# PSUM banks dealt out anew in a hybrid attention and matrix-memory block

## The chip, the cores and the metric

The kernel runs on one core of a Trainium2 chip. Its time is the device time of one execution in microseconds (us); lower is better. In tables and rows, PE is TensorE's matmuls, PEld its weight loads, DVE is VectorE, ACT is ScalarE, POOL is GpSimd, and SP is the engine that issues most of the DMA transfers; a name such as SPq or PEq is that engine's instruction queue. L12 is line 12 of the kernel before the change. In the changed kernel the same statement stands one line higher from line 316 on, since one line is gone; the text keeps the numbers of before, except where rows of the new order are shown.

## The reference

The input x is 1024 tokens by 1024 channels. It is normalised and multiplied by one wide matrix, whose columns feed two branches and their gates:

```
xn = rmsnorm(x);  da_q, da_k, da_v, da_z, ml_q, ml_k, ml_v, ml_o, ml_z, ml_i, ml_f, gate_a, gate_m = split(xn @ w_in)

# differential attention, 8 heads, two score maps p of 64 columns each
probs[p] = softmax(mask(q[p] @ k[p].T / 8 + bias))        # block-causal mask, 64-token chunks
y_a = rmsnorm((probs[0] - lam * probs[1]) @ v) * silu(da_z)

# mLSTM, 8 heads, chunkwise: decayed state C = C * decay + (w * k).T @ v
h = (scores @ v + w_inter * (q @ C)) / max(|den|, exp(-m))
y_m = sigmoid(ml_o) * layernorm(h) * silu(ml_z)

merged = sigmoid(gate_a) * (y_a @ w_pa) + sigmoid(gate_m) * (y_m @ w_pm)
out = rmsnorm(x + merged @ w_out)
```

All in float32. The kernel keeps that precision on TensorE by splitting each operand of the large products into two 16-bit parts, a high and a low half, and running three matmuls for each product (high by high, high by low, low by high).

## The kernel before

**Units.** The wide product is done in units of 256 columns. A unit's weights are loaded (`load`, L226, on SP's queue) into two tiles `wt`, of which three exist, and prepared (`prep`): ScalarE squares them (L245), VectorE adds the sums (L159), a matmul with a matrix of ones (L165) adds over the partitions, VectorE derives a power-of-two scale `sb` from it (`pow2`, L135 to L139), and four times ScalarE writes a high half (L257) and VectorE a low half (L259). Then TensorE multiplies: `plain_unit` (L329 to L331, 96 matmuls of 512 columns, called projection matmuls below) or `rows_unit` (L358 to L360, 192 matmuls of 256 columns). Each unit has 32 steps (`yield`). In each step one step of the next unit's preparation is written, too.

**Sides.** Beside the units of a phase runs a side: attention of the head before, or `mlstm` of the head before. A side is cut into named pieces, and a table (`PLAN_A` for the first seven attention heads, `PLAN_C` for the eighth, others for mlstm) gives each piece the slot of its writing. In `attention`, `q` and `r` are the scores (L812) and softmax (L822, L826) of a row block of 128 tokens for the two maps. `r` also combines them (L832 to L837), splits the result into halves (L844 on ScalarE, L845 on VectorE) and transposes it by a DMA (L847, tile z). `v` is the product of the transposed block with v (L855 to L857, then a square on ScalarE, L858); `f` makes the norm factors of four row blocks on GpSimd (L862 to L864); `o` scales their products (L870, reads PSUM); `t` turns the rows for the later projection (L547 to L549).

**PSUM.** Eight banks in four pools: `pp` three for the units, `psb` one tile of two banks for scores, `pmi` two for everything small, `pvp` one for the products with v. Four row blocks share one bank of `pvp`: it is taken by row blocks 0 and 4.

```
        def pv(i):
            if i % 4 == 0:
                ops[i // 4] = v_ps()
```

**What sets the order.** The code's order gives priorities. A scheduler of the programming layer then places the instructions of each engine in a fixed order by its own model, and lets a tile wait until a buffer of its pool is free. Each engine and each DMA queue executes its own list in order.

**The start.** `startup` transposes x block by block into PSUM (L396) and splits it (L398 on ScalarE, L399 on VectorE), woven with the first unit's preparation. `tables` writes the bias table to DRAM (L430, L432); its reader is `strip` (L584). The first unit is q and k of head 0, whose halves are copied to Q and K by DMA (L608, L610), the second v and z of head 0. `if_proj` writes the matrix-memory gates (L468, L471 on ScalarE, L472 on SP).

Of the kernel before, what the change touches and what calls it, by code (L numbers as in the profile page):

```python
# [17 lines left out]
P = 128  # L18
# [14 lines left out]
OFF_GATE = (9232, 10256)  # L33
BIG = 3.0e38
RING = 15
PLAN_A = [(0, 'q0'), (0, 'r0'), (0, 'q1'), (3, 'r1'), (4, 'q2'), (5, 'r2'), (9, 'q3'), (9, 'r3'), (9, 'q4'), (10, 'v0'), (14, 'v1'), (16, 'r4'), (17, 'q5'), (18, 'v2'), (19, 'r5'), (21, 'q6'), (24, 'r6'), (25, 'q7'), (27, 'r7'), (28, 'v3'), (29, 'v4'), (29, 'v5'), (30, 'f0'), (30, 'o0'), (31, 'v6'), (31, 'v7'), (42, 't0'), (55, 'f1'), (55, 'o1'), (55, 't1')]
PLAN_C = [(0, 'q0'), (0, 'r0'), (6, 'q1'), (7, 'r1'), (7, 'q2'), (9, 'r2'), (16, 'q3'), (19, 'r3'), (19, 'q4'), (19, 'r4'), (19, 'v0'), (22, 'v1'), (22, 'v2'), (25, 'q5'), (28, 'r5'), (29, 'q6'), (31, 'v3'), (32, 'v4'), (33, 'r6'), (37, 'q7'), (38, 'f0'), (38, 'r7'), (46, 'o0'), (52, 'v5'), (52, 'v6'), (63, 'v7'), (64, 'f1'), (67, 'o1'), (82, 't1'), (83, 't0')]
PLAN_M = [(0, '00gate'), (0, '01k0'), (2, '02k1'), (4, '03s0'), (5, '04s1'), (8, '05e0'), (9, '06p0'), (11, '07e1'), (13, '08p1'), (14, '09c0'), (19, '10g00'), (19, '11g01'), (20, '12g02'), (21, '13cp0'), (22, '14bs0'), (22, '15g10'), (25, '16g11'), (25, '17g12'), (26, '18cp1'), (30, '19bs1'), (30, '20g20'), (30, '21g21'), (31, '22cp2'), (32, '23bs2'), (33, '24ch'), (37, '25n0'), (47, '26t0'), (50, '27n1'), (55, '28t1')]
PLAN_N = [(0, '00gate'), (1, '01k0'), (1, '02k1'), (8, '03s0'), (10, '04s1'), (13, '05e0'), (13, '06p0'), (15, '07e1'), (16, '08p1'), (22, '09c0'), (25, '10g00'), (26, '11g01'), (26, '12g02'), (26, '13cp0'), (30, '14bs0'), (31, '15g10'), (36, '16g11'), (37, '17g12'), (40, '18cp1'), (42, '19bs1'), (43, '20g20'), (44, '21g21'), (53, '22cp2'), (54, '23bs2'), (59, '24ch'), (61, '25n0'), (67, '26t0'), (70, '27n1'), (71, '28t1')]
# [9 lines left out]
def block_kernel(ctx, tc, x, norm_w, w_in, lam, subln_w, rel_bias, conv_w, conv_b, b_if,  # L49
# [3 lines left out]
    PSUM = bass.MemoryType.PSUM  # L53
# [6 lines left out]
    dram = ctx.enter_context(tc.tile_pool(name="dram", bufs=1, space=bass.MemoryType.DRAM))  # L60
    pp = ctx.enter_context(tc.tile_pool(name="pp", bufs=3, space=PSUM))
    psb = ctx.enter_context(tc.tile_pool(name="psb", bufs=1, space=PSUM))
    pmi = ctx.enter_context(tc.tile_pool(name="pmi", bufs=2, space=PSUM))
    pvp = ctx.enter_context(tc.tile_pool(name="pvp", bufs=1, space=PSUM))

    uid = [0]

# [166 lines left out]
    def prep(w, rowscale=None, keep=False):  # L234
        wd = w.width
        if rowscale is not None:
            g.tensor_tensor(w.wt[0], w.wt[0], rowscale[:, 0:4].unsqueeze(2).to_broadcast([P, 4, wd]), op=ALU.mult)
            yield
            for k in range(4, 8):
                s.activation(w.wt[k // 4][:, k % 4, :], w.wt[k // 4][:, k % 4, :], AF.Copy, scale=rowscale[:, k:k + 1])  # L240
            yield
        ss = sm(cols=2, p="wss")
        for k in range(2):
            j = junk(4 * wd).rearrange("p (a b) -> p a b", a=4)
            s.activation(j, w.wt[k], AF.Square, accum_out=ss[:, k:k + 1])  # L245
            yield
        yield
        yield
        w.sb = sm(p="sb")
        w.isb = sm(p="isb", bufs=8)  # L250
        fnorm_finish(ss, w.sb, w.isb)
        yield
        w.parts = {}

        def split(name, src, dst):
            w.parts[name] = dst
            s.activation(dst[0], src, AF.Copy, scale=w.sb)  # L257
            yield
            v.scalar_tensor_tensor(dst[1], src, w.sb, dst[0], op0=ALU.mult, op1=ALU.subtract)  # L259
            yield  # L260

        if keep:
            t = [R(F16, [P, KC, 256], p="wo") for _ in range(2)]
        for k in range(0, KC, 2):
            src = w.wt[k // 4][:, k % 4:k % 4 + 2, :]
            if keep:
                dst = (t[0][:, k:k + 2, :], t[1][:, k:k + 2, :])
            else:
                u = wparts([2, 256])
                dst = (u[:, 0, :, :wd], u[:, 1, :, :wd])  # L270
            yield from split(k // 2, src, dst)
# [25 lines left out]
    class Unit:  # L297
# [13 lines left out]
        def start_prep(self):  # L311
            if self.prepping is None:
                self.finish_load()
                self.prepping = prep(self.w, self.rowscale and self.rowscale(), self.keep)
                self.left = 16

        def prep_step(self):
            return spent(self.prepping)
# [71 lines left out]
    def startup(th):  # L390
        for kc in range(KC):
            if kc % 2 == 0:
                X[th, kc // 2] = xtile("X")
            tp = m_ps()
            for tt in range(4):
                te.transpose(tp[:, tt * P:(tt + 1) * P], xts[th * 4 + tt][:, kc * P:(kc + 1) * P], ident)  # L396
            hi, lo = x_src(kc, th)
            s.activation(hi, tp, AF.Copy, scale=nws[:, kc:kc + 1])  # L398
            v.scalar_tensor_tensor(lo, tp, nws[:, kc:kc + 1], hi, op0=ALU.mult, op1=ALU.subtract)  # L399
            yield  # L400
# [49 lines left out]
    def if_proj():  # L450
# [11 lines left out]
            yield  # L462
        t = R(shape=[32, S], p="gif")
        for th in range(2):
            gps = m_ps()
            for i in range(KC):
                for k in range(2):
                    te.matmul(gps[:32, :], parts[:, i, :], x_src(i, th)[k], start=(i + k == 0),  # L468
                              stop=(i + k == KC))
                yield  # L470
            s.activation(t[:, HS[th]], gps[:32, :], AF.Copy, scale=sig[:32, :])  # L471
# [3 lines left out]
    def if_gates():  # L475
# [51 lines left out]
        s.dma_start(dec_d[0:1, :].rearrange("o (h c) -> (o h) c", c=NT), dec)  # L527
        s.dma_start(decb, dec_d[0:1, :].to_broadcast([P, H * NT]))
        yield
        cps = m_ps()  # L530
        for k, t in enumerate((a, ws, en)):
            for c in range(NT):
                o = (k * NT + c) * H
# [354 lines left out]
    def mlstm(h):  # L888
# [6 lines left out]
        kw = R(shape=[P, NT, P], p="kw")  # L895
        for th in range(2):
            n = 4 - th
            tp = m_ps()
            for j in range(n):
                c = th * 4 + j  # L900
                te.transpose(tp[:, j * P:(j + 1) * P], k[:, c * P:(c + 1) * P], ident)
# [320 lines left out]
```

## Time and profile before

| | us |
|---|---|
| median of 3 runs (lowest to highest) | 1435.84 (1435.15 to 1436.73) |
| the profiled execution, its own time | 1435.78 |
| its span, from first to last instruction | 1433.9 |
| mean granted TensorE clock | 0.995 |
| TensorE busy, DVE busy, ACT busy, POOL busy | 1380.6, 848.0, 735.0, 157.5 |
| share of the chain that ended last: PE, DVE, ACT, DMA, POOL | 77%, 9%, 4%, 4%, 3% |

Matmuls overlap, so TensorE's busy time is the union of theirs. A row of the timeline gives start, duration, engine, line, operation, output and inputs, shape, count, and in brackets how long the engine stood before it and what ended that. A row of the waits gives who waited on whom, total us, times and the longest. A row of busy times by stretch gives the stretch, its length, the busy time of PE, PEld, DVE, ACT and POOL with counts, the granted clock (1.00 is full), the DMA share and GB/s.

### The profile page before, as it was taken

How to read it: one execution, taken by the hardware profiler on the slowest of the kernel's cores; microseconds unless marked ns; L12 is line 12 of the kernel's file. 1: busy time of each engine (PE TensorE's matmuls, PEld its weight loads, DVE VectorE, ACT ScalarE, POOL GpSimd, SP SyncE). 2: the span in 40 equal slices, each digit the busy share in tenths (PEclk: the TensorE clock that was granted, in tenths of full speed). 3: DMA queues.
4: the chain of work that ended last, by engine and by line, in shares of the span. 5: the costliest groups of instructions: out<-in, count | busy, mean ns of one | idle time of the engine just before them, and what ended most of it. 6: DMA issues, size and time to landing. Idle time of an engine off the chain costs nothing.

```text
span 1433.9 us, 25050 instructions
## 1 busy us (share of the span) xinstructions
PE 1380.6 (96%) x9650; PEld 913.3 (64%) x9650; DVE 848.0 (59%) x2310; ACT 735.0 (51%) x1533; POOL 157.5 (11%) x215
## 2 busy tenths in 40 slices
PE   6989999999999999999999999999999999999997
PEld 3656575665756655444486787778769675444786
DVE  6276868677686756533445674775866564233633
ACT  7276556565566667832353444443435344644542
POOL 2001010010100100100102020220211200122004
PEclk9999999999999999999999999999999999999999
DMA  6456355463554645543321313231232135534303
GB/s 200 68 142 140 83 107 124 104 141 82 114 121 91 136 95 130 163 149 125 96 74 60 104 31 101 47 87 47 66 97 75 60 86 158 168 103 162 118 16 118
DMA packets 232585, 150.14 MB, mean 105 GB/s; under 512 B 117297, under 2 KB 209730, under 8 KB 232466
## 3 DMA queue, kind: packets, MB, share of 16 engines
q1 hardware_dynamic: 218450, 123.28, 35.0%
q10 hardware_dynamic: 14016, 25.27, 5.3%
q8 instruction: 75, 1.23, 0.3%
q14 instruction: 44, 0.36, 0.1%
HBM read 90.12 MB, written 18.55 MB: 76 GB/s over the span
## 4 chain that ended last, share of the span: by engine, by line
PE 77%; DVE 9%; ACT 4%; DMA 4%; POOL 3%; issue 3%; SPq 0%; POOLq 0%; DVEq 0%; ACTq 0%
PE pp L329 14%; PE pp L331 14%; PE pp L330 14%; PE pp L360 8%; PE pp L358 8%; PE pp L359 8%; PE psb L812 3%; DVE z L822 3%; DMA z<-z 2%; ACT z L826 1%; DMA qw<-rows_d 1%; DVE wp L259 1%; PE psb L908 1%; PE pvp L855 1%; DVE hl L600 1%
## 5 line engine op out<-in xcount | busy, mean ns | idle before, releaser
L358 PE MATMUL pp<-wp,X 128*128 128x256 f16 x1280 | 349.7, 273 | 0.0
L359 PE MATMUL pp<-wp,X 128*128 128x256 f16 x1280 | 349.7, 273 | 0.0
L360 PE MATMUL pp<-wp,X 128*128 128x256 f16 x1280 | 349.7, 273 | 0.0
L329 PE MATMUL pp<-X,wp 128*128 128x512 f16 x768 | 291.7, 380 | 0.3 <-ACT wp L257 0.3
L331 PE MATMUL pp<-X,wp 128*128 128x512 f16 x768 | 291.3, 379 | 0.6 <-DVE wp L259 0.6
L330 PE MATMUL pp<-X,wp 128*128 128x512 f16 x768 | 291.8, 380 | 0.0
L257 ACT ACTIVATE wp<-wt,sb 128x512 f16<-128x512 f32 x208 | 136.9, 711 | 105.4 <-DVE sb L138 70.6
L331 PEld LDWEIGHTS <-wp 128*128 128x128 f16 x1024 | 100.0, 98 | 119.7 <-DVE wp L259 1.2
L245 ACT ACTIVATE junk<-wt 128x1024 bf16<-128x1024 f32 x112 | 118.1, 1055 | 100.0 <-DMA wt<-in_w_in_dram 89.7
L329 PEld LDWEIGHTS <-wp 128*128 128x128 f16 x1024 | 100.2, 98 | 103.0 <-issue 1.7
L330 PEld LDWEIGHTS <-wp 128*128 128x128 f16 x1024 | 100.1, 98 | 97.1
L259 DVE SCALAR_TENSOR_TENSOR wp<-wt,sb,wp 128x512 f16<-128x512 f32 x208 | 150.5, 760 | 14.4 <-ACT wp L257 12.8
L359 PEld LDWEIGHTS <-X 128*128 128x128 f16 x1280 | 125.3, 98 | 18.4 <-issue 2.4
L358 PEld LDWEIGHTS <-X 128*128 128x128 f16 x1280 | 125.4, 98 | 16.8 <-issue 0.8
L360 PEld LDWEIGHTS <-X 128*128 128x128 f16 x1280 | 125.3, 98 | 14.6
L826 ACT ACTIVATE z<-z,mx 128x256 f32<-128x256 f32 (+7 forms) x128 | 99.0, 773 | 61.7 <-DVE mx L825 46.1
L822 DVE CUSTOM_DVE_ANT_0 z<-psb,BB,negc 128x256 f32<-128x256 f32 (+7 forms) x128 | 104.1, 813 | 19.7 <-PE psb L812 19.4
L331 PE MATMUL pp<-Y,wp 128*128 128x512 f16 x256 | 97.1, 379 | 0.0
L330 PE MATMUL pp<-Y,wp 128*128 128x512 f16 x256 | 97.1, 379 | 0.0
L329 PE MATMUL pp<-Y,wp 128*128 128x512 f16 x256 | 97.1, 379 | 0.0
L649 DVE SCALAR_TENSOR_TENSOR acc<-up,wcol,acc 128x512 f32<-128x512 f32 x96 | 78.0, 827 | 27.4 <-POOL acc L650 24.5
L812 PE MATMUL psb<-K,Q 128*128 128x512 f16 (+3 forms) x384 | 83.5, 326 | 7.8 <-DMA K<-hl 4.6
(245 smaller groups left out, 2012.1 us busy)
## 6 DMA issues: line engine op xcount, KB each, us to landing
wt<-in_w_in_dram SPq DMA_DIRECT2D x128, 256.0 KB, 3.4
wt<-in_w_in_dram SPq DMA_DIRECT2D x24, 512.0 KB, 3.9
K<-hl SPq DMA_DIRECT2D x32, 256.0 KB, 3.7
gate_d<-tg ACTq DMA_DIRECT2D x32, 256.0 KB, 2.2
xt<-in_x_dram SPq DMA_DIRECT2D x8, 512.0 KB, 5.2
Q<-hl SPq DMA_DIRECT2D x32, 128.0 KB, 2.4
wt<-in_w_pa_dram SPq DMA_DIRECT2D x8, 512.0 KB, 5.4
ft<-gate_d ACTq DMA_DIRECT2D x16, 256.0 KB, 2.8
```

The source lines that it names most:

```text
L245: s.activation(j, w.wt[k], AF.Square, accum_out=ss[:, k:k + 1])
L257: s.activation(dst[0], src, AF.Copy, scale=w.sb)
L259: v.scalar_tensor_tensor(dst[1], src, w.sb, dst[0], op0=ALU.mult, op1=ALU.subtract)
L329: te.matmul(ps, wh, xh, start=(start and i == 0), stop=False, **kw)
L330: te.matmul(ps, wh, xl, start=False, stop=False, **kw)
L331: te.matmul(ps, wl, xh, start=False, stop=(stop and i == n - 1), **kw)
L358: te.matmul(ps[:, o], xh[:, t], wh, start=i == 0, stop=False)
L359: te.matmul(ps[:, o], xh[:, t], wl, start=False, stop=False)
L360: te.matmul(ps[:, o], xl[:, t], wh, start=False, stop=i == KC - 1)
L812: te.matmul(sp[:, c:e], Q[:, p, i * P:(i + 1) * P], K[p][:, j, c:e], start=(j == 0), stop=(j == 1))
L822: v.tensor_tensor_reduce(z[:, :n], sp[:, :n], bb[:, S - n:], negc, BIG, op0=ALU.add, op1=ALU.min, accum_out=mx)
L826: s.activation(z[:, :n], z[:, :n], AF.Exp, bias=mx, scale=-1.0, accum_out=rr[:, 2 * i + p:2 * i + p + 1])
```

## The change

Of the eight banks, `pvp` gets two instead of one and `pmi` one instead of two. The transposes at the start, the gate products, and mlstm's transposes and state products move from `pmi` to `pvp`; `pmi` keeps the norm sums and three small uses at the start. The norm sum of a preparation stands three steps later. In `PLAN_A` the products with v of row blocks 6 and 7 stand two and four slots later. An unused line (`self.left`) is gone.

```
-PLAN_A = [... (30, 'f0'), (30, 'o0'), (31, 'v6'), (31, 'v7'), (42, 't0') ...]
+PLAN_A = [... (30, 'f0'), (30, 'o0'), (33, 'v6'), (35, 'v7'), (42, 't0') ...]
...
-    pmi = ctx.enter_context(tc.tile_pool(name="pmi", bufs=2, space=PSUM))
-    pvp = ctx.enter_context(tc.tile_pool(name="pvp", bufs=1, space=PSUM))
+    pmi = ctx.enter_context(tc.tile_pool(name="pmi", bufs=1, space=PSUM))
+    pvp = ctx.enter_context(tc.tile_pool(name="pvp", bufs=2, space=PSUM))
...
             s.activation(j, w.wt[k], AF.Square, accum_out=ss[:, k:k + 1])
             yield
-        yield
-        yield
+        for _ in range(5):
+            yield
         w.sb = sm(p="sb")
...
-            tp = m_ps()          # startup, transposes of x
+            tp = v_ps()
...
-            gps = m_ps()         # if_proj
+            gps = v_ps()
...
-        cps = m_ps()             # if_gates
+        cps = v_ps()
...
-            tp = m_ps()          # mlstm, transposes of k
+            tp = v_ps()
...
-            cp = m_ps()[:, :P + 1]   # mlstm, state
+            cp = v_ps()[:, :P + 1]
```

The scheduler's order changes with it at many places. Three are shown: the start, the start of attention (two engines), and one attention head.

*The start, VectorE.* X halves are L399 (now L398), x scaled is L387 (L386), low halves of the first weights L259. Before:

```order
L399 SCALAR_TENSOR_TENSOR X_214<-pmi_240,nws_134,X_214 128x512
L381 ISA junk_250,xss_249<-xt_104 128x1024
L399 SCALAR_TENSOR_TENSOR X_256<-pmi_257,nws_134,X_256 128x512
L387 TENSOR_SCALAR xt_104<-xt_104,xrs_252 128x1024
L259 SCALAR_TENSOR_TENSOR wp_247<-wt_156,sb_222,wp_247 128x512
L387 TENSOR_SCALAR xt_105<-xt_105,xrs_268 128x1024
L399 SCALAR_TENSOR_TENSOR X_256<-pmi_272,nws_134,X_256 128x512
L387 TENSOR_SCALAR xt_106<-xt_106,xrs_284 128x1024
L399 SCALAR_TENSOR_TENSOR X_288<-pmi_289,nws_134,X_288 128x512
L259 SCALAR_TENSOR_TENSOR wp_279<-wt_156,sb_222,wp_279 128x512
```

After:

```order
L398 SCALAR_TENSOR_TENSOR X_214<-pvp_229,nws_134,X_214 128x512
L380 ISA junk_237,xss_236<-xt_104 128x1024
L398 SCALAR_TENSOR_TENSOR X_243<-pvp_244,nws_134,X_243 128x512
L386 TENSOR_SCALAR xt_104<-xt_104,xrs_239 128x1024
L386 TENSOR_SCALAR xt_105<-xt_105,xrs_254 128x1024
L398 SCALAR_TENSOR_TENSOR X_243<-pvp_258,nws_134,X_243 128x512
L386 TENSOR_SCALAR xt_106<-xt_106,xrs_279 128x1024
L398 SCALAR_TENSOR_TENSOR X_283<-pvp_284,nws_134,X_283 128x512
L259 SCALAR_TENSOR_TENSOR wp_291<-wt_156,sb_265,wp_291 128x512
L398 SCALAR_TENSOR_TENSOR X_283<-pvp_293,nws_134,X_283 128x512
L259 SCALAR_TENSOR_TENSOR wp_309<-wt_156,sb_265,wp_309 128x512
```

The first low half of weights stood before the scaling of x block 105; now it stands four operations further on, behind the low half of pvp_284.

*The start of attention, TensorE.* L165 is the norm sum of the third unit, L812 (now L811) the score products of head 0: psb_923 and psb_931 are row block 0 in the two maps, psb_944 is row block 1; pp_843 is the last quarter of the second unit, 48 matmuls. Before:

```order
L360 MATMUL pp_790<-wp_523,X_394 128x256
L165 MATMUL pmi_705<-s_703,ones_91 128x1
L812 MATMUL psb_923<-K_426,Q_425 128x128
...
L812 MATMUL psb_931<-K_427,Q_425 128x128
...
L358 MATMUL pp_843<-wp_492,X_325 128x256
...
L812 MATMUL psb_944<-K_426,Q_425 128x256
```

After:

```order
L359 MATMUL pp_784<-wp_536,X_394 128x256
L165 MATMUL pmi_728<-s_726,ones_91 128x1
L811 MATMUL psb_923<-K_426,Q_425 128x128
...
L357 MATMUL pp_843<-wp_505,X_325 128x256
...
L811 MATMUL psb_931<-K_427,Q_425 128x128
...
L811 MATMUL psb_944<-K_426,Q_425 128x256
```

The second score product stood right behind the first; now the 48 matmuls of pp_843 stand between, and row block 1 follows with 7 projection matmuls of the third unit done instead of 3.

*The same place, ScalarE.* gif is the gates' product (L471, now L470), wp the high halves of the third unit, wt_669 and the tile after it the fourth unit's weights, mx_927 and mx_934 the softmax of row block 0 in the two maps. Before:

```order
L245 ACTIVATE junk_681,wss_672<-wt_532 128x1024
L471 ACTIVATE gif_600<-pmi_601,sig_443 32x512
L471 ACTIVATE gif_600<-pmi_619,sig_443 32x512
L567 ACTIVATE vr_644<-pp_650 128x256
L257 ACTIVATE wp_718<-wt_458,sb_701 128x512
L257 ACTIVATE wp_738<-wt_458,sb_701 128x512
...
L257 ACTIVATE wp_753<-wt_532,sb_701 128x512
L257 ACTIVATE wp_768<-wt_532,sb_701 128x512
...
L826 ACTIVATE z_926,rr_920<-z_926,mx_927 128x128
...
L826 ACTIVATE z_926,rr_920<-z_926,mx_934 128x128
L245 ACTIVATE junk_962,wss_961<-wt_669 128x1024
```

After:

```order
L245 ACTIVATE junk_681,wss_672<-wt_545 128x1024
L257 ACTIVATE wp_741<-wt_458,sb_724 128x512
...
L257 ACTIVATE wp_791<-wt_545,sb_724 128x512
L470 ACTIVATE gif_600<-pvp_601,sig_443 32x512
L470 ACTIVATE gif_600<-pvp_619,sig_443 32x512
...
L562 ACTIVATE tz_643<-pp_711,hs_640 128x256
L825 ACTIVATE z_926,rr_920<-z_926,mx_927 128x128
L245 ACTIVATE junk_962,wss_961<-wt_669 128x1024
L245 ACTIVATE junk_967,wss_961<-wt_806 128x1024
L562 ACTIVATE tz_643<-pp_843,hs_640 128x256
```

The four high halves moved ahead of the gates, and both squares (L245) of the fourth unit moved ahead of the second softmax of row block 0. On VectorE the small sum over these squares stands ahead of the scan of psb_931.

*An attention head (the second), VectorE.* z_1984 and z_2003 belong to row block 6, z_2022 and z_2038 to row block 7, on_2151 is the scaling of row blocks 0 to 3 (L870, now L869), hl halves of the next head's k. Before:

```order
L600 SCALAR_TENSOR_TENSOR hl_1880<-pp_1975,hl_1880 128x512
L834 SCALAR_TENSOR_TENSOR nbeta_2008<-rr_1694,nlam_141,rc_1695 128x1
L837 SCALAR_TENSOR_TENSOR z_1984<-z_2003,nbeta_2008,z_1984 128x896
L822 ISA z_2038,mx_2039<-psb_2033,BB_95,negc_899 128x1024
L845 TENSOR_TENSOR z_2003<-z_1984,z_2003 128x896
L870 SCALAR_TENSOR_TENSOR on_2151<-pvp_1855,fac_2147,tz_1289 128x128 x2
L832 RECIPROCAL rc_1695<-rr_1694 128x2
L870 SCALAR_TENSOR_TENSOR on_2151<-pvp_1855,fac_2147,tz_1289 128x128
L834 SCALAR_TENSOR_TENSOR nbeta_2043<-rr_1694,nlam_141,rc_1695 128x1
L870 SCALAR_TENSOR_TENSOR on_2151<-pvp_1855,fac_2147,tz_1289 128x128
L837 SCALAR_TENSOR_TENSOR z_2022<-z_2038,nbeta_2043,z_2022 128x1024
```

After:

```order
L836 SCALAR_TENSOR_TENSOR z_1984<-z_2003,nbeta_2008,z_1984 128x896
L821 ISA z_2038,mx_2039<-psb_2033,BB_95,negc_899 128x1024
L844 TENSOR_TENSOR z_2003<-z_1984,z_2003 128x896
L599 SCALAR_TENSOR_TENSOR hl_1874<-pp_1975,hl_1874 128x512
L831 RECIPROCAL rc_1695<-rr_1694 128x2
L869 SCALAR_TENSOR_TENSOR on_2151<-pvp_1850,fac_2147,tz_1289 128x128
L833 SCALAR_TENSOR_TENSOR nbeta_2043<-rr_1694,nlam_141,rc_1695 128x1
L869 SCALAR_TENSOR_TENSOR on_2151<-pvp_1850,fac_2147,tz_1289 128x128
L836 SCALAR_TENSOR_TENSOR z_2022<-z_2038,nbeta_2043,z_2022 128x1024
L869 SCALAR_TENSOR_TENSOR on_2151<-pvp_1850,fac_2147,tz_1289 128x128 x2
```

The hl half moved from ahead of row block 6's combination to behind its low half, and the small factor nbeta_2043 of row block 7 from behind the third scaling to behind the first. On TensorE, 6 instead of 37 projection matmuls (L358 to L360) stand between the products of row blocks 3 and 4 of this head, and 66 instead of 71 between those of row blocks 3 and 7. On ScalarE the squares L858 of row blocks 4 and 5 stand ahead of row block 7's high half as one of them did before, with one L245 more.

More of the change, by code (lines that the diff above doesn't have):

```diff
@@ L35 @@
 RING = 15
-PLAN_A = [(0, 'q0'), (0, 'r0'), (0, 'q1'), (3, 'r1'), (4, 'q2'), (5, 'r2'), (9, 'q3'), (9, 'r3'), (9, 'q4'), (10, 'v0'), (14, 'v1'), (16, 'r4'), (17, 'q5'), (18, 'v2'), (19, 'r5'), (21, 'q6'), (24, 'r6'), (25, 'q7'), (27, 'r7'), (28, 'v3'), (29, 'v4'), (29, 'v5'), (30, 'f0'), (30, 'o0'), (31, 'v6'), (31, 'v7'), (42, 't0'), (55, 'f1'), (55, 'o1'), (55, 't1')]
+PLAN_A = [(0, 'q0'), (0, 'r0'), (0, 'q1'), (3, 'r1'), (4, 'q2'), (5, 'r2'), (9, 'q3'), (9, 'r3'), (9, 'q4'), (10, 'v0'), (14, 'v1'), (16, 'r4'), (17, 'q5'), (18, 'v2'), (19, 'r5'), (21, 'q6'), (24, 'r6'), (25, 'q7'), (27, 'r7'), (28, 'v3'), (29, 'v4'), (29, 'v5'), (30, 'f0'), (30, 'o0'), (33, 'v6'), (35, 'v7'), (42, 't0'), (55, 'f1'), (55, 'o1'), (55, 't1')]
 PLAN_C = [(0, 'q0'), (0, 'r0'), (6, 'q1'), (7, 'r1'), (7, 'q2'), (9, 'r2'), (16, 'q3'), (19, 'r3'), (19, 'q4'), (19, 'r4'), (19, 'v0'), (22, 'v1'), (22, 'v2'), (25, 'q5'), (28, 'r5'), (29, 'q6'), (31, 'v3'), (32, 'v4'), (33, 'r6'), (37, 'q7'), (38, 'f0'), (38, 'r7'), (46, 'o0'), (52, 'v5'), (52, 'v6'), (63, 'v7'), (64, 'f1'), (67, 'o1'), (82, 't1'), (83, 't0')]
@@ L314, in start_prep @@
                 self.prepping = prep(self.w, self.rowscale and self.rowscale(), self.keep)
-                self.left = 16
         def prep_step(self):
```

## The prediction

> **What bounds the kernel now.** I read the page's first table, then TensorE's part of the table of waits, then the busy times by stretch, and last the timeline of the stretches where TensorE stands. Busy shares first:
>
> ```profile
> span 1433.9 us, 25050 instructions
> PE 1380.6 (96%) x9650; PEld 913.3 (64%) x9650; DVE 848.0 (59%) x2310; ACT 735.0 (51%) x1533; POOL 157.5 (11%) x215
> 760.00:880.00 120.00, 120.00 (x911) 91.61 (x910) 78.13 (x223) 52.12 (x106) 16.21 (x20) 1.00 0.26 71
> 160.00:220.00 60.00, 56.73 (x444) 38.07 (x442) 43.94 (x126) 37.44 (x86) 4.61 (x8) 1.00 0.54 110
> ```
>
> In the last two rows the first number after the stretch is its length, the second TensorE's busy time. In 760 to 880 us (the matrix-memory heads) TensorE never stands, so nothing is to be won there. In one attention head (160 to 220) it stands 3.3 us of 60. What it stands for:
>
> ```profile
> PE pvp L855 <- DVE on L870: 12.0, 8, 1.6
> PE psb L812 <- DMA K<-hl: 4.6, 2, 2.5
> PE pvp L855 <- DMA z<-z: 4.2, 5, 1.1
> PE pmi L165 <- DVE s L159: 1.6, 7, 0.2
> ```
>
> Columns: total us, times, longest. The first row is the single bank of pvp: the fifth product with v (row block 4, L855) waits until the scaling L870 has read the first four out of it, once per head. The third is the last product with v, which waits for its transposed probabilities. The fourth is the norm sum, a matmul placed before its input is there. The second is one place, the start of attention. Together 22.4 us; the kernel is TensorE's work plus these, so a gain is read in TensorE's waits alone.
>
> **The change part by part.** One head in detail (the second; the others look alike):
>
> ```profile
> 176.73 1.28 DVE L822 CUSTOM_DVE_ANT_0 z<-psb,BB,negc 128x1024 f32<-128x1024 f32 x1 [1.11 <-PE psb L812]
> 180.96 0.35 ACT L858 ACTIVATE junk<-pvp,rc 128x128 bf16<-128x128 f32 x1
> 181.30 1.14 ACT L826 ACTIVATE z<-z,mx 128x1024 f32<-128x1024 f32 x1
> 183.51 0.20 POOL L864 TENSOR_TENSOR fac<-fac,rc 128x4 f32<-128x4 f32 x1
> 183.75 0.61 DVE L870 SCALAR_TENSOR_TENSOR on<-pvp,fac,tz 128x128 f32<-128x128 f32 x2 [1.53 <-POOL fac L864]
> 184.98 1.28 DVE L837 SCALAR_TENSOR_TENSOR z<-z,nbeta,z 128x1024 f32<-128x1024 f32 x1
> 185.12 0.22 PE L855 MATMUL pvp<-vr,z 128*128 128x128 f16 x1 [1.59 <-DVE on L870]
> 186.57 1.04 ACT L844 ACTIVATE z<-z 128x1024 f16<-128x1024 f32 x1
> 187.65 1.23 DVE L845 TENSOR_TENSOR z<-z,z 128x1024 f16<-128x1024 f32 x1 [0.58 <-ACT z L844]
> 187.72 0.27 PE L358 MATMUL pp<-wp,X 128*128 128x256 f16 x1
> 187.83 0.27 PE L359 MATMUL pp<-wp,X 128*128 128x256 f16 x1
> 188.90 4.91 DMA z<-z
> 193.86 0.23 PE L855 MATMUL pvp<-vr,z 128*128 128x128 f16 x1 [0.98 <-DMA z<-z]
> ```
>
> *Second bank for pvp.* The product of row block 4 no longer waits for L870. That removes 1.59 us here and 12.0 us in all eight heads. In the new order it also stands earlier: 6 instead of 37 projection matmuls lie between row blocks 3 and 4. The work is the same, only its place differs.
>
> *What is late next.* The path to the last product (row block 7) is softmax L826 (ends 182.5), L837 (184.98), the high half L844, the low half L845, and the transposing DMA, 4.91 us, landing at 193.81. TensorE will now be there sooner: by 1.59, by 0.24 for the norm sum (below), and by 0.55, since 66 instead of 71 projection matmuls, 0.11 us apart (187.72 to 187.83), stand between row blocks 3 and 7; 2.4 us. If the landing stayed, the wait of 0.98 would become 3.3. Does it move? Three things in the new orders say yes. L837's small factor stands behind the first L870 instead of the third, so L837 starts about 0.5 sooner after the factor of L864. L844 no longer stands behind a square L858 that waits for the late product, and starts as L837 ends: 0.35. And the score products of row block 7 stand 4 projection matmuls (0.86 us) earlier on TensorE, and L600 no longer stands ahead of row block 6's L837 (0.6 us): of these I count 1.25 us together, since VectorE stood 1.11 us for those scores (176.73). Sum 2.1 us, against TensorE's 2.4. So the wait stays about what it is, and of the third row (4.2 us) I book neither gain nor loss. Placing row blocks 6 and 7 two and four slots later adds nothing of its own: on TensorE's queue row block 7 still stands after nearly the same work. Bounds: the wait goes altogether, 4.2 more; only the 0.85 of the first two reasons come true, then it grows by 1.5 in seven heads, 10.5 less.
>
> *A page that speaks against it.* The Trainium skill (TensorE: Matmul & The Clock Gate, section "HAM oscillation — how this bites in real kernels") reports a kernel whose TensorE waited for transferred data, where double-buffering PSUM brought no further gain. By that the 12.0 us would turn up behind the transposing DMA, and the sum below would come out at about 1438. The third row of the waits agrees that such a wait stands right behind the removed one, at a third of its size.
>
> *Norm sums on a bank of their own, three steps later.* The matmul L165 then finds its input: 1.6 us of waits go. Nobody needs the prepared weights sooner: the preparation takes 16 of a unit's 32 steps instead of 13, and in 760 to 880, where nothing waits now, a unit's weights are ready with half a unit to spare. I cost the later step at nothing there; if that cover failed, L329 or L358 would wait for L257. The other uses (transposes of the keys, state products) take the two pvp banks as they took the two of pmi: nothing.
>
> *The start is where it costs.* Two places.
>
> ```profile
> 21.18 0.75 DVE L259 SCALAR_TENSOR_TENSOR wp<-wt,sb,wp 128x512 f16<-128x512 f32 x1
> 25.17 0.74 DVE L259 SCALAR_TENSOR_TENSOR wp<-wt,sb,wp 128x512 f16<-128x512 f32 x1
> 21.99 0.39 PE L331 MATMUL pp<-X,wp 128*128 128x512 f16 x1 [0.63 <-DVE wp L259]
> 22.22 0.38 PE L329 MATMUL pp<-X,wp 128*128 128x512 f16 x1
> 34.12 0.40 DVE L430 TENSOR_SCALAR tb<-tb 8x384 f32<-8x384 f32 x1
> 34.55 0.82 SPq L432 DMA_DIRECT2D tb_d<-tb  x1
> 69.22 0.35 SPq L584 DMA_DIRECT2D strip<-tb_d  x1
> ```
>
> The first weights' norm sum comes three rounds later, so VectorE makes their first low half (L259 at 21.18) behind four more operations, about where the second stands now (25.17). TensorE, which runs without a break from 21.99, starts that run near 25.9. By then it has done 15 projection matmuls now and 4 in the new order, with as many transposes: 11 at 0.22 us apart (21.99 to 22.22), 2.4 us late. I take 2.3, between 1.5 (if VectorE packs closer) and 3.5 (two norm sums in one bank follow closely there). The bias table's write (L432) gets about 1.4 us sooner, since its source L430 now stands ahead of operations that wait for ScalarE; its reader (strip, L584) waits for it until 69.22, and the keys behind it on SP's queue.
>
> ```profile
> 72.46 1.06 ACT L245 ACTIVATE junk<-wt 128x1024 bf16<-128x1024 f32 x1 [20.93 <-DMA wt<-in_w_in_dram]
> 73.52 1.23 ACT L471 ACTIVATE gif<-pmi,sig 32x512 f32<-32x512 f32 x2
> 74.23 0.16 PE L165 MATMUL pmi<-s,ones 128*128 128x1 bf16 x1 [0.50 <-ACT gif L471]
> 75.05 1.33 ACT L257 ACTIVATE wp<-wt,sb 128x512 f16<-128x512 f32 x2
> 75.22 1.16 SPq L472 DMA_DIRECT2D gif_d<-gif  x1
> 76.43 2.80 SPq L226 DMA_DIRECT2D wt<-in_w_in_dram  x4
> 76.86 0.37 PE L812 MATMUL psb<-K,Q 128*128 128x128 f16 x2 [2.47 <-DMA K<-hl]
> 79.34 0.37 PE L812 MATMUL psb<-K,Q 128*128 128x128 f16 x2 [2.10 <-DMA K<-hl]
> 80.00:82.00 2.00, 2.00 (x11) 1.40 (x10) 2.00 (x8) 1.72 (x7) 0.00 (x0) 0.50 1.08 299
> 82.00:84.00 2.00, 2.00 (x18) 1.64 (x16) 0.88 (x4) 1.06 (x3) 0.00 (x0) 0.85 1.12 304
> 86.92 0.38 PE L812 MATMUL psb<-K,Q 128*128 128x256 f16 x2
> wt<-in_w_in_dram SPq DMA_DIRECT2D x128, 256.0 KB, 3.4
> ```
>
> Now TensorE waits 0.50, 2.47 and 2.10 us here, and after it the granted clock is 0.50 (third number from the end of the row 80 to 82; 0.85 in 82 to 84, so until about 82.6). In the new order it comes to L165 at 73.73 + 2.3 = 76.0, after the keys, so these three waits go; a unit of 48 matmuls then stands ahead of the second score product. But ScalarE now does the four L257 ahead of the gates L471, and these need the norm sum: L257 from 76.85 (0.82 after L165, as now) to 79.5, L471 to 80.7. On SP's queue the gates' write (1.2) stands ahead of the next weights, whose last part is issued at 84.0 and lands 3.4 later, 87.4. Behind it in order: L245 (1.25, to 88.65), the norm's small sum, the v copy and the low half (0.7), the scan L822 of the second score product, which frees the only psb: the third score product runs at about 89.8, now at 86.92. TensorE will stand some 6 us there. Against now: 2.9 us later, less 4 matmuls (0.9) done ahead, plus 1.6 for 3.2 us at half clock once more, which now lies inside the 86.92. A loss of 3.6 us. Bounds: 0 (weights land sooner, a shorter delay before) and 6 (a delay of 3.5, more of the clock).
>
> **Sum.** 12.0 + 1.6 - 3.6 = 10.0 us less. The profiled execution took 1435.78 us (span 1433.9 and 1.9 around it), 0.06 under the median of the runs, 1435.84: 1425.8, said as 1426.
>
> **The rivals.**
> First, the wait moves to the transposing DMA: if row block 7 lands only 0.85 us sooner, a head keeps 0.3 us; seven heads 2.1, the eighth's 1.5, less 3.6: 1436, no change. For it: the 4.91 us DMA and the chain ahead of it are not shortened; against it: VectorE's 1.11 us stand for the scores. From there on it decides the sign: if it lands no sooner at all, each head loses 0.55 (the 5 matmuls that now stand behind), 3.9 in seven, plus 3.6 less 1.5: 1442, slower.
> Second, that wait goes too, row block 7 having slots to spare: 1426 less 4.2, 1421.6.
> Third, the start costs nothing: 1422.3. For it: the three waits of 5.1 us do go; against it the queue of SP told above.
> Fourth, between the forecast and the first: half of the landing's gain, about 1431.
> That the change doesn't do what it says is excluded by the new order, where row block 4 stands ahead of L870.
>
> **How the numbers follow.** Forecast (1423 to 1429) 0.50; second rival 0.15; third 0.13; fourth 0.07; no change at 1436 0.09; slower at 1442 0.06. A measurement tells about 0.2%, 2.9 us, from no change. Faster: 0.50 + 0.15 + 0.13 + 0.07 = 0.85; same 0.09; slower 0.06. The range, 1420 to 1433, leaves out the last two (0.15) and a little below; it takes in either bound of the start and half the upper bound of the landing.
>
> **What would show it.** Right: the wait on L870 gone from TensorE's table; L855 on the transposed z at 3 to 7 us; L165 on s near 0; a stand of 5 to 7 us on psb near 84 to 90 us, ended by L822; attention heads 1.5 to 2 us shorter each; the stretch of the matrix-memory heads unchanged. Wrong: L855 waiting 10 us or more for z; no stand near 85; new waits of L329 or L358 for L257.

## The result: 1.0% slower, and the profile after

In what follows the changed kernel's rows bear its own line numbers from 316 on (L870 is L869, L951 is L950), and those of the experiments with added lines one or two more.

The changed kernel takes 1452.08 us (median of 4 runs, 1446.73 to 1453.36) against 1435.92 before (4 runs beside them): a ratio of 1.0104, 95% interval 1.0089 to 1.0118. The forecast was 1426, range 1420 to 1433. The profiled execution took 1452.28 us. The page's head:

```profile
span 1450.2 us, 25053 instructions
PE 1383.5 (95%) x9650; PEld 917.1 (63%) x9650; DVE 847.7 (58%) x2310; ACT 737.1 (51%) x1533; POOL 159.1 (11%) x215
```

The busy times of the stretch that was shown of before:

```profile
760.00:880.00 120.00, 116.55 (x882) 88.52 (x881) 76.95 (x223) 52.30 (x106) 16.10 (x20) 1.00 0.27 71
```

Where TensorE never stood, it now stands 3.45 us. The same view over whole stages (stretch, its length, TensorE's busy time; the third number from the end is the granted clock), of before:

```profile
0.00:100.00 100.00, 80.58 (x466) 47.71 (x467) 53.09 (x170) 53.00 (x103) 12.13 (x32) 0.97 0.57 135
100.00:525.00 425.00, 404.01 (x3129) 270.02 (x3127) 311.99 (x877) 264.19 (x601) 31.73 (x54) 1.00 0.53 112
760.00:1240.00 480.00, 479.11 (x3439) 346.62 (x3438) 294.67 (x859) 213.39 (x420) 60.34 (x70) 1.00 0.30 84
```

and of after:

```profile
0.00:100.00 100.00, 76.25 (x446) 47.00 (x447) 48.34 (x152) 49.22 (x94) 11.80 (x32) 0.95 0.55 132
100.00:525.00 425.00, 409.65 (x3166) 274.39 (x3165) 318.38 (x899) 269.73 (x614) 31.65 (x54) 1.00 0.55 114
760.00:1240.00 480.00, 464.01 (x3340) 337.98 (x3339) 290.02 (x854) 203.25 (x401) 58.15 (x69) 1.00 0.29 78
```

The length less the busy time is TensorE's standing: at the start 19.4 before and 23.8 after, in attention 21.0 and 15.4, in the matrix-memory heads 0.9 and 16.0. So +4.3, -5.6 and +15.1; with 2.9 us more of TensorE's busy time (1383.5 against 1380.6), 0.2 less in 525 to 760 and 0.2 less behind 1240 that is the 16.3 between the spans.

The 2.9 us go with a slower clock. Before, the granted clock is clearly under 1 while TensorE works in one place (74 to 84 us); after, it is in four (24 to 30, 82 to 88, 432 to 436 and 1024 to 1030 us). An estimate, busy time times what the clock lacks in rows of 2 us, gives 1.8 us lost before and 6.2 after. That is 4.3 more, of which 1.4 do not show in the busy time; why is open. The last of the four places lies in the matrix-memory heads, behind a stand of 2.26 us for num:

```profile
1026.00:1028.00 2.00, 2.00 (x9) 1.38 (x9) 1.37 (x6) 0.11 (x1) 1.79 (x2) 0.50 0.01 2
```

TensorE's waits:

```profile
PE psb L944 <- ACT num L950: 9.9, 5, 2.7
PE pvp L854 <- DMA z<-z: 8.9, 8, 2.5
PE pp L357 <- DVE tz L563: 7.3, 1, 7.3
PE psb L946 <- DVE C L929: 4.9, 6, 0.9
PE psb L946 <- issue: 1.2, 2, 0.9
PE pvp L854 <- ACT wp L257: 2.1, 2, 1.0
```

The waits on L870 and of L165 on s are gone, as forecast. The first, fourth and fifth row are all matrix-memory heads and make up their 16.0: L944, a product of scores with v, waits for num, ScalarE's copy of the three products before it, and L946, the product with the state C, waits for VectorE's update of C. No L328 or L357 waits for L257 there: the weights themselves are in time.

**Where the 15 us come from.** One unit's preparation in the first of these heads, by the timeline. TensorE does L165, VectorE L135 to L139 (the scale) and L259, ScalarE L257; then follow the load L226 of the next weights and their squares L245. Before:

```profile
760.25 1.05 PE L908 MATMUL psb<-acc,acc 128*128 128x128 f32 x8
763.33 0.17 PE L165 MATMUL pmi<-s,ones 128*128 128x1 bf16 x1
764.51 0.15 DVE L138 TENSOR_SCALAR sb<-nb 128x1 int32<-128x1 int32 x1
767.87 1.69 SPq L226 DMA_DIRECT2D wt<-in_w_in_dram  x3
774.16 1.06 ACT L245 ACTIVATE junk<-wt 128x1024 bf16<-128x1024 f32 x1 [1.31 <-DMA wt<-in_w_in_dram]
775.69 0.49 ACT L951 ACTIVATE num<-psb 128x387 f32<-128x387 f32 x1 [0.38 <-PE psb L947]
777.66 0.39 PE L945 MATMUL psb<-vr,E 128*128 128x129 f32 x2
```

After:

```profile
756.97 1.05 PE L907 MATMUL psb<-acc,acc 128*128 128x128 f32 x8
761.99 0.17 PE L165 MATMUL pmi<-s,ones 128*128 128x1 bf16 x1
763.25 0.75 DVE L648 SCALAR_TENSOR_TENSOR acc<-up,wcol,acc 128x512 f32<-128x512 f32 x1
764.71 0.15 DVE L138 TENSOR_SCALAR sb<-nb 128x1 int32<-128x1 int32 x1
767.55 2.02 SPq L226 DMA_DIRECT2D wt<-in_w_in_dram  x3
771.99 0.39 PE L946 MATMUL psb<-C,qw 128*128 128x129 f32 x2
773.07 1.06 ACT L245 ACTIVATE junk<-wt 128x1024 bf16<-128x1024 f32 x1 [4.68 <-DMA wt<-in_w_in_dram]
774.46 1.06 ACT L245 ACTIVATE junk<-wt 128x1024 bf16<-128x1024 f32 x1 [0.24 <-DMA wt<-in_w_in_dram]
775.52 0.47 ACT L950 ACTIVATE num<-psb 128x387 f32<-128x387 f32 x1
776.04 0.49 PE L944 MATMUL psb<-vr,E 128*128 128x129 f32 x2 [1.50 <-ACT num L950]
```

Counted from the first score product (L908, then L907): the norm sum stands at 3.1 before and 5.0 after, which are the three steps; the last step of the scale but one (L138) comes at 4.3 and 7.7, since VectorE now does convolutions (L648, 0.75 each) among its steps; the load of the next weights is issued at 7.6 and 10.6, as VectorE is done with a tile; the second square starts at 13.9 and 17.5, both after standing for the landing (1.31 before; 4.68 and 0.24 now); num is copied at 15.4 and 18.6. Before, num's copy waited for its products (0.38), and the next product came 1.5 us after num was done, so nothing was seen of all this. Now the last of its products (L946) is done at about 772.4, the copy starts 3.1 us later, behind both squares, and TensorE stands 1.50 us. Nothing is late for the weights; the squares are late for ScalarE's queue. VectorE's queue stands too: its sum over the squares (L159, at 774.26) waits 3.25 us for the first of them, and two updates of C stand behind it (774.34). In every second head the same chain reaches TensorE by a longer way (timeline of after):

```profile
824.77 1.06 ACT L245 ACTIVATE junk<-wt 128x1024 bf16<-128x1024 f32 x1 [1.40 <-DMA wt<-in_w_in_dram]
826.51 2.04 POOL L649 TENSOR_SCALAR acc<-up,wcol,cols 128x512 f32<-128x512 f32 x2 [13.89 <-ACT up L344]
827.31 0.75 DVE L648 SCALAR_TENSOR_TENSOR acc<-up,wcol,acc 128x512 f32<-128x512 f32 x1 [3.74 <-POOL acc L649]
827.98 0.29 DVE L932 COPY C<-pvp 128x129 f32<-128x129 f32 x1
830.18 0.49 PE L946 MATMUL psb<-C,qw 128*128 128x129 f32 x2 [0.91 <-DVE C L929]
```

Behind the squares stands the copy of q and k (L344), GpSimd's part of the convolution waits for it (13.89 us idle before it), VectorE's part for that (3.74), and behind it on VectorE stand the state's copy L932 and update, for which L946 waits.

### The profile page after: what moved, and what is told of

Read it like the earlier page. It is cut to its first block, busy times and chain, and to the rows that moved or that the text cites. A ratio compares the mean times of both kernels' runs of the same rounds, so it can differ in the third digit from the quotient of the medians.

```text
span 1450.2 us, 25053 instructions
## 1 busy us (share of the span) xinstructions
PE 1383.5 (95%) x9650; PEld 917.1 (63%) x9650; DVE 847.7 (58%) x2310; ACT 737.1 (51%) x1533; POOL 159.1 (11%) x215
## 4 chain that ended last, share of the span: by engine, by line
PE 72%; DVE 9%; ACT 5%; DMA 5%; issue 5%; POOL 3%; SPq 0%; POOLq 0%; DVEq 0%; ACTq 0%
PE pp L328 12%; PE pp L330 12%; PE pp L329 12%; PE pp L357 9%; PE pp L358 8%; PE pp L359 8%; PE psb L811 3%; DMA z<-z 3%; DVE z L821 2%; DVE acc L648 1%; DMA wt<-in_w_in_dram 1%; ACT z L825 1%; ACT wp L257 1%; DMA qw<-rows_d 1%; DVE z L844 1%
## 5 line engine op out<-in xcount | busy, mean ns | idle before, releaser
L357 PE MATMUL pp<-wp,X 128*128 128x256 f16 x1280 | 349.7, 273 | 7.3 <-DVE tz L563 7.3
L358 PE MATMUL pp<-wp,X 128*128 128x256 f16 x1280 | 349.7, 273 | 0.0
L328 PE MATMUL pp<-X,wp 128*128 128x512 f16 x768 | 292.5, 381 | 0.0
L257 ACT ACTIVATE wp<-wt,sb 128x512 f16<-128x512 f32 x208 | 135.8, 712 | 80.4 <-DVE sb L138 58.0
L245 ACT ACTIVATE junk<-wt 128x1024 bf16<-128x1024 f32 x112 | 118.3, 1056 | 114.6 <-DMA wt<-in_w_in_dram 102.8
L328 PEld LDWEIGHTS <-wp 128*128 128x128 f16 x1024 | 100.5, 98 | 101.9 <-issue 2.3
L259 DVE SCALAR_TENSOR_TENSOR wp<-wt,sb,wp 128x512 f16<-128x512 f32 x208 | 146.9, 751 | 19.1 <-ACT wp L257 17.7
L357 PEld LDWEIGHTS <-X 128*128 128x128 f16 x1280 | 125.6, 98 | 23.7 <-DVE tz L563 7.5
L358 PEld LDWEIGHTS <-X 128*128 128x128 f16 x1280 | 125.5, 98 | 15.8
L648 DVE SCALAR_TENSOR_TENSOR acc<-up,wcol,acc 128x512 f32<-128x512 f32 x96 | 80.8, 858 | 43.7 <-POOL acc L649 41.6
L328 PE MATMUL pp<-Y,wp 128*128 128x512 f16 x256 | 97.0, 379 | 0.0
L811 PE MATMUL psb<-K,Q 128*128 128x512 f16 (+3 forms) x384 | 83.2, 325 | 3.8 <-DVE mx L821 3.3
```

Of the source, the lines that this page charges most:

```text
L328: te.matmul(ps, wh, xh, start=(start and i == 0), stop=False, **kw)
L357: te.matmul(ps[:, o], xh[:, t], wh, start=i == 0, stop=False)
L358: te.matmul(ps[:, o], xh[:, t], wl, start=False, stop=False)
L811: te.matmul(sp[:, c:e], Q[:, p, i * P:(i + 1) * P], K[p][:, j, c:e], start=(j == 0), stop=(j == 1))
```

## The experiments

Theory A: the later norm sums cost the matrix-memory heads, by the chain above. Rival B: the new banks for their key transposes and state products do. The runs are against the kernel before on the same chip.

**Later norm sums alone** (late_only):

```
 # kernel before
-        yield
-        yield
+        for _ in range(5):
+            yield
         w.sb = sm(p="sb")
```

> The kernel before with one part of the change alone: five steps instead of two ahead of the norm sum. Theory A (the later norm sums cost the matrix-memory heads: weight tiles come free later, their loads come later, ScalarE's square L245 stands at the head of its queue for them, and the copy num L951 behind it keeps TensorE's next product L945 waiting): the loss of the changed kernel shows here, 10 to 20 us between the first and the last state product of the heads, TensorE waits of L945 for num of 8 to 12 us, and the time is 1446 to 1460. Theory B (the loss comes from putting the key transposes and state products on the two banks of pvp): no such waits, time 1434 to 1440, the few us being the start.

Measured: 1450.61 us, ratio 1.0108 (1.0095 to 1.0122). TensorE waits 6.1 us for num, less than the 8 to 12 expected, and 5.5 for C; its busy times:

```profile
100.00:525.00 425.00, 409.58 (x3164) 273.43 (x3162) 317.57 (x893) 269.22 (x614) 34.04 (x54) 1.00 0.54 115
760.00:1240.00 480.00, 464.94 (x3348) 337.58 (x3346) 290.18 (x854) 204.95 (x406) 57.95 (x69) 1.00 0.29 79
```

With the old banks the heads stand 15.1 us. A holds. In attention the same step alone already takes the standing from 21.0 to 15.4, as much as the whole change does.

**Banks and slots without the later norm sums** (banks_plan), **and banks alone** (banks_only):

```
 # changed kernel
-        for _ in range(5):
-            yield
+        yield
+        yield
 # banks_only besides: PLAN_A with (31, 'v6'), (31, 'v7') again
```

> The changed kernel with two steps again ahead of the norm sum: the banks and the two slots of row blocks 6 and 7 are changed, the norm sums are not. Theory A: TensorE's waits for num fall from 9.9 us to under 2, the matrix-memory heads take what they took before, the attention heads keep their gain of about 8 us, the start costs less than 3 us: 1424 to 1431. Theory B: the waits for num stay at 8 to 12 us and the time at 1446 to 1455.

> As the run before, and row blocks 6 and 7 back in slot 31: only the banks are changed. If the slots matter, the last product with v now stands earlier on TensorE than its transposed block lands, and its wait for z grows by 1 to 3 us in each of seven heads: 7 to 20 us above the run with the new slots. If they do not (the scheduler places the product by its own model), the two agree within 2 us. On the matrix-memory heads theories A and B expect what they expect of the run with the new slots.

Measured: 1433.59 us, ratio 0.9986 (0.9977 to 0.9995), and 1432.32, ratio 0.9979 (0.9970 to 0.9988). From the first of the two, a row of the busy times and two of TensorE's waits:

```profile
760.00:1240.00 480.00, 479.33 (x3434) 345.64 (x3433) 295.79 (x864) 216.35 (x425) 60.38 (x70) 1.00 0.30 85
```

```profile
PE pmi L165 <- DVE s L159: 9.2, 7, 1.6
PE pp L357 <- DVE tz L563: 7.3, 1, 7.3
```

The heads stand 0.7 us: B falls, the banks cost them nothing. The slots do nothing either: by TensorE's timeline 19 projection matmuls stand between row blocks 5 and 6 and 38 between 6 and 7 in both kernels, in the first six heads, and the intervals overlap. But the gain is 2 to 3 us and not 10: the wait on L870 has gone, and the norm sum L165 now waits 9.2 us for its input s in attention. The expected 1424 to 1431 missed this.

**A fourth weight tile** (after_wt4):

```
-WT = 3
+WT = 4
```

> The changed kernel with four weight tiles wt instead of three, norm sums still three steps later. Theory A, with the tile as the link: a load no longer waits for the tile that the later preparation frees, L245 finds its weights, TensorE's waits for num fall from 9.9 to under 3 us, time 1430 to 1438 (the start keeps its cost). Rival A2 (the later norm sum itself, not the tile: VectorE's and ScalarE's queues merely stand in a worse order) and theory B: the waits stay, 1445 to 1455.

Measured: 1453.26 us, ratio 1.0123 (1.0106 to 1.0140); TensorE's waits for num are 9.0 us. The timeline of the same place in the first head:

```profile
765.31 2.02 SPq L226 DMA_DIRECT2D wt<-in_w_in_dram  x2
769.14 1.06 ACT L245 ACTIVATE junk<-wt 128x1024 bf16<-128x1024 f32 x1 [2.99 <-DMA wt<-in_w_in_dram]
772.21 1.06 ACT L245 ACTIVATE junk<-wt 128x1024 bf16<-128x1024 f32 x1 [1.91 <-DMA wt<-in_w_in_dram]
```

So the tile is not what holds the squares up, as I had it. The squares ahead of num are now those of one tile further on (L159, the sum over a unit's two squares, stands behind the second of the two and no longer behind the first); their load is again issued about as VectorE releases a tile, and they wait for its landing again. That the scheduler puts squares as early as its model lets them is my reading and not shown; what the next run shows is that they are the link.

**Squares that wait for nothing** (sq_resident):

```
+        w.ml = unit.kind in ("mqk", "mz", "mvo")
...
+            src = ones[:, 0:1].unsqueeze(2).to_broadcast([P, 4, wd]) if w.ml else w.wt[k]
-            s.activation(j, w.wt[k], AF.Square, accum_out=ss[:, k:k + 1])
+            s.activation(j, src, AF.Square, scale=1.0 / 32 if w.ml else 1.0,
+                         accum_out=ss[:, k:k + 1])
```

> The changed kernel, but in the units of the matrix-memory heads ScalarE squares a tile of ones that is always there (scaled so that the sum is about that of the weights) in place of the weights just loaded: the sums of the weights are left out there, every instruction else stays, and the norm sums stand in the same places among the projection matmuls as in the changed kernel. Theory A' (the loss is the square L245, which stands first in ScalarE's queue until the weights land; the later norm sum frees the weight tile later and so makes the landing late against num): the stands of TensorE in 760 to 1240 us fall from 16 us to under 3, time 1433 to 1439. Rival A2 (the squares are innocent: the later scale, VectorE's convolutions ahead of it and the later halves are what delays num and C): 10 us or more of the stands stay, time 1446 to 1452.

Measured: 1436.09 us, ratio 1.0008 (0.9999 to 1.0017): 16.0 less than the changed kernel. What is left is 2.3 us for num:

```profile
760.00:1240.00 480.00, 477.73 (x3416) 344.78 (x3415) 293.45 (x858) 199.03 (x393) 60.70 (x70) 1.00 0.30 83
```

The standing falls from 16.0 to 2.3 us, though the norm sums are as late as ever: in the first head L165 comes 5.0 us and the scale (L138) 7.7 us behind the first score product, as in the changed kernel, so A2 falls. A' holds: the later norm sum acts through the squares' place at the head of ScalarE's queue. The run does not part their wait from their place, since with nothing to wait for both squares also moved ahead of the four high halves (763.86 and 765.04, against 766.10). The Trainium skill (TensorE: Matmul & The Clock Gate, the table at its head) calls the queues of ScalarE, VectorE and GpSimd strictly first in, first out; the changed kernel's trace agrees, num's copy of 0.47 us starting 1.06 after the second square.

**Later norm sums in the matrix-memory units only** (late_ml) **and in attention only** (late_da):

```
+        w.late = 5 if unit.kind in ("mqk", "mz", "mvo") else 2               # late_ml
+        w.late = 5 if unit.kind in ("aqk", "avz") and unit.idx else 2        # late_da
...
-        for _ in range(5):
+        for _ in range(w.late):
```

> The changed kernel with five steps ahead of the norm sum in the units of the matrix-memory heads only (mqk, mz, mvo), two in all others. Theory A: the whole loss of those heads is here, 15 to 18 us above the run with two steps everywhere (1433.6): 1448 to 1452. If a part of the loss came from the late norm sums of other units (start, attention, gates, last projections), it is below 1445.

> The changed kernel with five steps only in the attention units of heads 1 to 7, two in all others. Theory A: matrix-memory heads as before the change, no stand for num. In attention the wait of L165 on s (9.2 us with two steps) goes, but the last product with v then comes sooner to its transposed block and its wait for z grows from 2.4 to about 8 to 10 us: 1431 to 1434, hardly better than with two steps. Rival (the transposed block has slots to spare): the 9 us come out of the time, 1424 to 1427.

Measured: late_ml 1452.94 us, ratio 1.0124 (1.0109 to 1.0139), the whole loss and 0.9 above the range expected. late_da 1430.42, ratio 0.9968 (0.9956 to 0.9981), a little better than expected, for the reason expected (TensorE's waits):

```profile
PE pvp L855 <- DMA z<-z: 10.8, 10, 2.7
```

L165 no longer waits for s in attention, and the wait for the transposed block is 10.8 us (2.4 in banks_plan, where L165 waited 9.2). With the second bank it is this landing that limits the attention heads: the wait ahead of it, taken away, comes back behind it.

**The gate products back on pmi** (gps_pmi, from banks_only):

```
-            gps = v_ps()
+            gps = m_ps()
```

> Only the banks changed (two steps, old slots; 1432.3), but the gate products at the start stay on the bank of pmi, as before the change, so that the third unit's norm sum L165 has to wait for the copy L470 and the four high halves L257 stand behind it. Theory S (the stand of 7.3 us of L357 near 75 us comes from the four L257 going ahead of the gates' copy on ScalarE): the stand goes, and what is left is a wait for the keys of about 5 us as before: 1428 to 1431. Rival (the stand is ScalarE's and VectorE's work there, in whatever order): it moves to another instruction, 1431 to 1434.

Measured: 1429.68 us, ratio 0.9961 (0.9948 to 0.9973). The stand is gone, and not even a wait for the keys is left, but the waits of the score products (L811) on the scan grow from 3.8 to 6.8 us; 18.7 us of standing up to 100 us against 21.2, and the clock stays full (busy times):

```profile
0.00:100.00 100.00, 81.29 (x478) 48.04 (x479) 53.76 (x172) 53.44 (x105) 12.13 (x32) 1.00 0.58 139
```

**Both remedies** (da_gps)**, and the last products later** (da_gps_v7, da_gps_v7a):

```
 # da_gps: late_da with gps = m_ps();  da_gps_v7 besides:
-(33, 'v6'), (35, 'v7'), (42, 't0')
+(36, 'v6'), (42, 'v7'), (44, 't0')      # da_gps_v7a: (34, 'v6'), (39, 'v7'), (42, 't0')
```

> Both remedies together: five steps ahead of the norm sum only in the attention units of heads 1 to 7 (1430.4 alone, 3.2 us under the run with two steps everywhere) and the gate products back on pmi (1429.7 alone, 2.6 us under the run with only the banks changed). If they add up: 1427 to 1429, with the wait of the last product with v on z still at 8 to 11 us. If the start's gain is used up in the first attention head: 1429 to 1431.

> As the run before, and the products with v of row blocks 6 and 7 in slots 36 and 42, the turning of the rows in 44: 43 instead of 19 projection matmuls of 0.11 us stand between the two, some 2.6 us. Theory W (what is left of the removed wait on L870 stands behind the landing of row block 7's transposed block, 0.9 to 2.7 us a head, and TensorE has other work for that time): the wait of the last product with v on z falls from about 10 us to under 3, 1418 to 1422. Rival (the later product holds up what comes after it: the bank, the factors, the rows of the next unit): the wait comes back elsewhere, 1426 to 1429.

> As the run before with slots 34 and 39: 25 instead of 19 projection matmuls stand between row blocks 6 and 7, 0.7 us. Theory W: the wait on z falls by 0.7 us in each of seven heads, about 5 us, 1422 to 1424. Rival: no change, 1426 to 1429.

Measured: da_gps 1429.67 us (runs between 1426.25 and 1429.89, both sides of the two expectations, so whether the remedies add up is not decided), ratio 0.9942 (0.9930 to 0.9955); da_gps_v7a 1424.27, ratio 0.9915 (0.9902 to 0.9929); da_gps_v7 1414.27 (1413.07 to 1414.97), ratio 0.9843 (0.9830 to 0.9857). The last beats both kernels, by 1.6% and 2.6%.

```profile
100.00:525.00 425.00, 408.50 (x3171) 273.21 (x3170) 316.14 (x892) 267.68 (x611) 31.57 (x54) 1.00 0.55 114
```

This was the busy time of da_gps in attention, and this is da_gps_v7's:

```profile
100.00:525.00 425.00, 419.21 (x3254) 281.12 (x3252) 322.78 (x911) 277.06 (x632) 38.64 (x57) 1.00 0.55 116
```

The standing in attention falls from 16.5 to 5.8 us, and the waits of L855 on z (8.2 us in da_gps) are gone from the table. Theory W holds. The gain is more than the 8 us expected: 2.7 us at the same product that are put down to the copy L258 went too. The cover is also more than I had counted. By TensorE's timeline the 43 instead of 19 projection matmuls stand between row blocks 5 and 6, not 6 and 7, and 42 instead of 36 stand between 6 and 7; so in heads 2 to 7 the last product stands 30 later, some 3.3 us and not 2.6. In da_gps_v7a it stands 6 later. Its median is 0.3 above where W put it, but in its profiled execution (1430.15 us) the two waits fall by 2.0 us (from 10.9 to 8.9) and not by 5, so its gain is not explained by them.

**The same without the second bank** (one_bank: the kernel before with late_da's steps and the slots 36, 42, 44):

> The kernel before with its banks as they were (one for the products with v, two for everything small), and of the last version only the later norm sums in the attention units of heads 1 to 7 and the slots 36, 42 and 44. Theory W2 (the second bank and the later slots are worth something only together: the bank takes the wait on L870 away, the slots give the landing cover): the wait on L870 stays, 41 instead of 37 projection matmuls stand ahead of it, so about 0.4 us less of it in each head, 9 of 12 us, and the time is 1427 to 1433. Rival (the later slots alone do it, the second bank is not needed): the wait on L870 falls under 4 us and the time is 1415 to 1421.

Measured: 1426.72 us, ratio 0.9946 (0.9932 to 0.9959). From TensorE's waits:

```profile
PE pvp L856 <- DVE on L871: 8.8, 8, 1.5
```

The wait on the single bank stays, 8.8 us; steps and slots alone are worth 8.5. From here to da_gps_v7 it is 12.4 us by the medians, and 13.8 with each against the kernel before on its own chip (1435.22 and 1436.54). The start's remedy is 2.6 of it (gps_pmi against banks_only), so 9.8 to 11.2 are the bank's, at least that wait. The bank's gain was there to be had, once the last product had cover; the cover, steps and slots together, was worth nearly as much.

## Why the prediction was wrong, point by point

- *The wait on L870, 12.0, and of L165 on s, 1.6:* both went. Right.
- *The last product with v stays as it is (4.2):* too low. By the second head, counted from its first scan of scores, in before

```profile
147.85 0.35 DVE L822 CUSTOM_DVE_ANT_0 z<-psb,BB,negc 128x128 f32<-128x128 f32 x1
```

and in after, with the issue of the transposing DMA (L846) and the last product:

```profile
150.67 0.35 DVE L821 CUSTOM_DVE_ANT_0 z<-psb,BB,negc 128x128 f32<-128x128 f32 x1
189.52 3.58 SPq L846 DMA_TRANSPOSE z<-z  x1
195.05 0.23 PE L854 MATMUL pvp<-vr,z 128*128 128x128 f16 x1 [1.83 <-DMA z<-z]
```

TensorE came 2.48 us sooner (195.05 less 1.83, against 193.86 less 0.98), forecast 2.4. The transposing DMA was issued 2.20 sooner (189.52, against 188.90), forecast 2.1. But from its issue to the product it took 5.53 us instead of 4.96, so the product could start only 1.63 sooner, and the wait grew by 0.85. The step took the transfer's time as fixed, and one head for all. What else the transfer met can be seen: three copies of k (K<-hl) were issued at 185.48, just ahead of it, and the DMA share was 0.92 and 0.76 in 189 to 191 us, where before it was 0.26 and 0.06 in 188 to 190. VectorE's half of k, from which they copy, stands later than before (183.58, against 178.02); the prediction counted that move as a gain alone. That the copies slowed the block is likely and not tested.

Over all heads 8.9 us stand behind z and 2.1 at the same product under L257's name, where 4.2 and 0.5 were; of the 13.6 us that went, a net gain of 5.6 is left in 100 to 525 us. From its first scan to that of the third the second head is 1.1 us shorter (59.79 against 60.88), forecast 1.5 to 2. That is the first rival, at more than half strength. The observation of the Trainium skill that the prediction cited (TensorE: Matmul & The Clock Gate, section "HAM oscillation — how this bites in real kernels"), no further gain from double-buffering PSUM in a kernel of that section, was half borne out by the change as made. It no longer was once the landing had cover (one_bank against da_gps_v7).
- *Norm sums three steps later, costed at nothing in the matrix-memory heads:* this step failed, 15.1 us. The cover that I named, weights ready half a unit ahead, held; L328 and L357 wait for nothing in these heads. I asked who waits for the weights and not what else the preparation releases: the weight tile, with it the next load, and with that the squares, which stand in ScalarE's queue ahead of num and of the convolutions' input. In the profile of before their waits on the DMA could be seen (1.31 us ahead of num), with 1.5 us of slack behind it.
- *State products and transposes on pvp, nothing:* right (banks_plan stands 0.7 us).
- *The start, 3.6:* about right. Up to 100 us there are 4.3 more of standing; at the second head's first scan the kernel is 2.8 us late (150.67, against 147.85), with the first head's gain, about 1.1 if it is as the second's, already in it. The order on ScalarE came as told, four L257 ahead of the gates (timeline, then a row of the busy times):

```profile
77.07 2.56 ACT L257 ACTIVATE wp<-wt,sb 128x512 f16<-128x512 f32 x4 [5.91 <-DVE sb L138]
79.53 1.23 ACT L470 ACTIVATE gif<-pvp,sig 32x512 f32<-32x512 f32 x2
83.86 0.40 PE L357 MATMUL pp<-wp,X 128*128 128x256 f16 x1 [7.29 <-DVE tz L563]
```

```profile
82.00:84.00 2.00, 0.14 (x1) 0.13 (x2) 1.25 (x6) 1.99 (x5) 0.00 (x0) 0.50 0.83 222
```

TensorE stood 7.29 us, a little more than the 5 to 7 forecast, but on a bank of pp that L563 had to read, behind ScalarE's queue, and not on psb behind L822. The clock fell to 0.50 there, as forecast. The cause of this stand was the gates' bank rather than the later norm sum: banks_plan stands 7.3 too, late_only and gps_pmi do not. The start as a whole has both causes: up to 100 us TensorE stands 21.5 in late_only and 21.9 in banks_plan, against 19.4 before and 23.8 after.

The sum: 15.1 for the heads, 8.0 less gained in attention (5.6 of 13.6), 0.7 more at the start (4.3 of standing; the 1.6 for the clock that the forecast's 3.6 had in it is in the next term here) and 2.9 of busy time, less the 0.2 in 525 to 760, make 26.5 (0.2 less behind 1240 us and 0.2 more outside the span cancel), as lie between 1425.8 and the profiled 1452.28.

## What to carry to other kernels

When a step of a preparation is moved, follow what it releases, not only what it delivers: the buffer, the next load into it, and the first instruction on that load, which may stand at the head of an engine's queue ahead of work that has nothing to do with it. A wait that is removed is worth what lies between it and the next arrival; give that arrival cover in the same change (here the product's slot), or most of the gain stands behind it. A buffer shared between two uses is also an order between them: giving each its own let four copies go ahead of the one that was needed.

## What the runs showed of the hardware

The transposing DMA of one and the same block took 4.96 us in one kernel and 5.53 in the other, from its issue to the product that waits for it; in the second the DMA engines were busy as it was issued (share 0.92, against 0.06 to 0.26). After 7.29 us of standing the granted clock was 0.50, as it had been after two stands of 2.47 and 2.10 us before. In the changed kernel it was 0.50 also behind single stands of 2.54 us (ended at 432.18) and 2.26 us (1025.68), but 1.00 behind one of 2.71 us (1201.24). So the length of a stand did not decide it alone, and what else does is open.
